# Program order for the casts and subtractions of left forms, with six buffers for forms and four for raw weights

## Chip, core and metric

The kernel runs on one core of one Trainium2 chip. The metric is the device time of one execution in microseconds, given as the median over runs; before the change it is 2421.71 us (three runs, 2420.68 to 2421.89).

## What is computed

One layer of a decoder trunk: three token mixers in parallel, a cross-attention, a gated feed-forward part and a last RMSNorm, on 1024 tokens of width 1024, in float32. The change touches only the first half of the feed-forward part:

```python
def conv_gated_ffn(h, w_up, conv_w, conv_b, w_down):
    u, v = jnp.split(h @ w_up, 2, axis=-1)          # 1024 x 1024 by 1024 x 5632
    u = causal_depthwise_conv(u, conv_w, width=3) + conv_b
    return (jax.nn.silu(u) * v) @ w_down
```

## The kernel before

Every float32 product is made of three products of rounded parts: an operand is split into a high part (`fp32r`, a cast on ScalarE) and a low part (operand minus high part, a subtraction), and high x high, high x low and low x high are summed in PSUM.

The up-projection is `ffn_up`. It treats `h @ w_up` as a two by two block product and uses a seven-product scheme: the seven right-hand forms `X` (B11, B21, T1, T2, T3, T4, B22, each as high and low part) are made from the normalised activations at the end of `trunk` and stay in SBUF. The left-hand forms come from the weights. For every block `f` of 128 columns (22 of them, D_FF/128) two raw tiles are loaded, `r1` from the u half and `r2` from the v half, 512 KB each; their halves are A11, A12, A21, A22, and GpSimd makes the sums S1, S2, S3, S4 out of them (line 1308, four per block). `left` yields one form after the other: it casts the block or sum on ScalarE (line 1315), and VectorE or GpSimd in turn subtracts (line 1316). `prod` runs the twelve matmuls of one product (line 1323).

`pair(f)` makes the products of block f and what follows them: T2 with S2 into bank `b`, T3 with S3 into half `c` of a two-bank tile `cd`, T1 with S1 into half `d`, T4 with A22 into `c` again, B22 with S4 into `d` again. VectorE reads these out between (lines 1384, 1386, 1388, 1393, 1395), then come the convolution (1397 to 1399), SiLU (1400), the gate (1401), and the left operands for the down-projection (1404, 1411 to 1413). For blocks 0 to 5 the two remaining products, A11 with B11 and A12 with B21, are made earlier by `ahead(f)`, while the end of the trunk still runs, and their results lie in DRAM (`part`); so those pairs have five products, the pairs 6 to 21 seven. After `ffn_up` comes `ffn_down`.

Buffers: the forms lie in four buffers, two of tag `whi` and two of `wlo`, taken in turn. Raw weights use two buffers of tag `raw` and, of the eight tiles r0 to r7 of another pool, r4 and r5 in the ahead stage, r2 to r5 in the pairs. r0 and r1 hold `y`, r6 and r7 hold `vt`. Before the up-projection r0 to r7 hold trunk tiles; r0 to r3 are reused there for the normalised rows from which the last right-hand forms, T3 and B22, are transposed.

The order of instructions on each engine is not written by hand. The framework schedules the program when it is built, by a simulated time line of its own: an instruction goes to its engine's queue when the simulation has it ready, and a buffer is handed out then too. Each engine then works through its queue in that fixed order. `issue_after(ins)` adds an edge that keeps what is issued inside it behind `ins` on the same engine.

Of the kernel before, what the change touches and what calls it, by code (L numbers as in the profile page):

```python
# [12 lines left out]
F32 = mybir.dt.float32  # L13
F32R = mybir.dt.float32r
# [3 lines left out]
ALU = mybir.AluOpType  # L18
# [3 lines left out]
P = 128  # L22
S = 1024
DM = 1024
NK = 8
OFF_HG, OFF_DA, OFF_RW, OFF_GATE, N_IN = 0, 2048, 3584, 5376, 8448
D_FF = 2816
NFF = 22
# [68 lines left out]
class K:  # L97
# [1194 lines left out]

    def left(self, r1, r2, which, sp):

        nc = self.nc
        V, A, G = nc.vector, nc.scalar, nc.gpsimd
        q = {f"A{n}{k + 1}": r[:, 4 * k:4 * k + 4, :] for n, r in ((1, r1), (2, r2)) if r is not None for k in range(2)}
        sums = {"S1": ("A21", "A22", ALU.add), "S2": ("S1", "A11", ALU.subtract), "S3": ("A11", "A21", ALU.subtract),  # L1300
                "S4": ("A12", "S2", ALU.subtract)}

        def get(n):
            if n not in q:
                a, b, op = sums[n]
                a, b = get(a), get(b)
                q[n] = sp.tile([P, 4, P], F32, tag=n, name=n, bufs=2 if n in ("S1", "S2") else 1)
                G.tensor_tensor(out=q[n], in0=a, in1=b, op=op)  # L1308
            return q[n]

        for n in which:
            x = get(n)
            self.nform = getattr(self, "nform", 0) + 1
            f = self.wp.tile([P, 2, 4, P], F32R, tag=("whi", "wlo")[self.nform % 2], name="wf")
            A.copy(out=f[:, 0], in_=x)  # L1315
            (V if self.nform % 2 else G).tensor_tensor(out=f[:, 1], in0=x, in1=f[:, 0].bitcast(F32), op=ALU.subtract)  # L1316
            yield f

    def prod(self, ps, f, x, start, stop):
        n = 0  # L1320
# [6 lines left out]
    def ffn_up(self, X, act, sums, part, spill):  # L1327


        nc, tc, I = self.nc, self.tc, self.I  # L1330
        V, A, G, T = nc.vector, nc.scalar, nc.gpsimd, nc.tensor
        with tc.tile_pool(name="up", bufs=1) as sp:
            col = lambda j, f: self.pc("ffn_conv_w", NFF * j + f) if j < 3 else self.pc("ffn_conv_b", f)
            nraw = itertools.count()
            u = sp.tile([P, S + 2], F32, name="u")
            G.memset(u[:, 0:2], 0.0)
            ne = part.shape[1]

            def load(m, bufs=6):
                n = next(nraw) % bufs  # L1340
                r = self.wp.tile([P, NK, P], F32, tag="raw", name="raw") if n < 2 else \
                    self.res.tile([P, NK, P], F32, tag=f"r{n + 6 - bufs}", name="raw")
                nc.sync.dma_start(out=r, in_=I["t_up"][m])
                return r

            def copy(nm, src):
                s1 = sp.tile([P, 512], F32, tag="s1", name=nm, bufs=3)
                A.copy(out=s1, in_=src)
                return s1

            def bank(f):
                return self.tps.tile([P, 512], F32, tag="t", name="ps_a") if f % 2 == 0 else \
                    self.dps.tile([P, 1024], F32, tag="d", name="ps_a")[:, 0:512]

            def ahead(f):
                forms, a = self.left(load(f, 4), None, ("A11", "A12"), sp), bank(f)
                self.prod(a, next(forms), X["B11"], True, True)
                nc.sync.dma_start(out=part[0, f], in_=copy("s1", a))
                yield
                self.prod(a, next(forms), X["B21"], False, True)  # L1360
                c = spill.tile([P, 512], F32, tag="acr", name="c11")
                A.copy(out=c, in_=a)
                nc.sync.dma_start(out=part[1, f], in_=c)
                yield

            def pair(f, rs):

                forms = self.left(*rs, ("S2", "S3", "S1", "A22", "S4") if f < ne else ("A11", "S2", "S3", "S1", "A12", "A22", "S4"), sp)
                if f < ne:
                    s1 = sp.tile([P, 512], F32, tag="s1", name="s1", bufs=3)  # L1370
                    nc.sync.dma_start(out=s1, in_=part[0, f])
                else:
                    a = self.tps.tile([P, 512], F32, tag="t", name="ps_a")
                    self.prod(a, next(forms), X["B11"], True, True)
                    s1 = copy("s1", a)
                if f < ne:
                    nc.sync.dma_start(out=u[:, 2:514], in_=part[1, f])
                vt = self.res.tile([P, S], F32, tag=f"r{6 + f % 2}", name="vt")
                b = self.mps.tile([P, 512], F32, tag="m", name="ps_b2")
                cd = self.dps.tile([P, 1024], F32, tag="d", name="ps_cd")  # L1380
                c, d = cd[:, 0:512], cd[:, 512:1024]
                u2, u3 = (sp.tile([P, 512], F32, tag=t, name=t) for t in ("u2", "u3"))
                self.prod(b, next(forms), X["T2"], True, True)
                V.tensor_tensor(out=u2, in0=b, in1=s1, op=ALU.add)
                self.prod(c, next(forms), X["T3"], True, True)
                V.tensor_tensor(out=u3, in0=c, in1=u2, op=ALU.add)
                self.prod(d, next(forms), X["T1"], True, True)
                V.tensor_tensor(out=vt[:, 512:1024], in0=d, in1=u3, op=ALU.add)
                if f >= ne:
                    self.prod(a, next(forms), X["B21"], False, True)  # L1390
                    A.copy(out=u[:, 2:514], in_=a)
                self.prod(c, next(forms), X["T4"], False, True)
                V.tensor_tensor(out=vt[:, 0:512], in0=c, in1=u2, op=ALU.add)
                self.prod(d, next(forms), X["B22"], False, True)
                V.tensor_tensor(out=u[:, 514:1026], in0=d, in1=u2, op=ALU.add)
                y = self.res.tile([P, S], F32, tag=f"r{f % 2}", name="y")
                A.activation(out=y, in_=u[:, 2:], func=AF.Identity, scale=col(2, f), bias=col(3, f))
                V.scalar_tensor_tensor(out=y, in0=u[:, 1:S + 1], scalar=col(1, f), in1=y, op0=ALU.mult, op1=ALU.add)
                V.scalar_tensor_tensor(out=y, in0=u[:, 0:S], scalar=col(0, f), in1=y, op0=ALU.mult, op1=ALU.add)
                A.activation(out=y, in_=y, func=AF.Silu)  # L1400
                V.tensor_tensor(out=y, in0=y, in1=vt, op=ALU.mult)
                q = nc.gpsimd if f >= NFF - 2 else nc.sync
                if f % 2 == 0:
                    V.tensor_tensor(out=y[:, 512:1024], in0=y[:, 0:512], in1=y[:, 512:1024], op=ALU.subtract)
                    even.append(y)
                q.dma_start(out=act[f], in_=y)
                if f % 2:
                    e = even.pop()
                    s2, s1, s4 = (self.res.tile([P, S], F32, tag=f"r{2 + n}", name="asum")[:, 0:512] if f == NFF - 1 else
                                  spill.tile([P, 512], F32, tag="acr", name="asum") for n in range(3))  # L1410
                    V.tensor_tensor(out=s2, in0=y[:, 512:1024], in1=e[:, 512:1024], op=ALU.subtract)
                    G.tensor_tensor(out=s4, in0=y[:, 0:512], in1=s2, op=ALU.subtract)
                    G.tensor_tensor(out=s1, in0=e[:, 0:512], in1=s2, op=ALU.add)
                    for n, x in enumerate((s2, s1, s4)):
                        q.dma_start(out=sums[n, f // 2], in_=x)

            even = []
            prev = None
            for f in range(ne):
                g = ahead(f)  # L1420
                next(g)
                if prev is not None:
                    next(prev)
                prev = g
            next(prev)
            rs = [load(0), load(NFF)]
            for f in range(NFF):
                nx = [load(f + 1), load(NFF + f + 1)] if f + 1 < NFF else None
                pair(f, rs)
                rs = nx  # L1430
# [200 lines left out]
```

## Time and profile before

| what | value |
|---|---|
| median of the runs | 2421.71 us (2420.68 to 2421.89) |
| profiled execution | 2418.76 us |
| its span, first to last instruction | 2417.0 us |
| mean granted clock of TensorE | 0.987 |
| PE busy | 2312.8 us, 96% |
| VectorE (DVE) busy | 1373.9 us, 57% |
| ScalarE (ACT) busy | 908.9 us, 38% |
| GpSimd (POOL) busy | 695.2 us, 29% |

The table is of one profiled execution. Busy matmul time is modelled, and neighbouring matmuls overlap in it, so starts of instructions say more than busy times. Times in the rows below are from the start of the span; the up-projection's products run from 1713 to 2188 us.

### The profile page before, as it was taken

The page shows a single profiled execution, that of the slowest core. Times are in us where ns is not written, and L with a number is a line of the kernel's source. Part 1 is how long each engine was busy: PE and PEld are TensorE (multiplying, and loading weights), DVE is VectorE, ACT ScalarE, POOL GpSimd, SP SyncE. Part 2 cuts the span into 40 slices and gives each one's busy share as a digit, 9 for nine tenths or more (in the row PEclk, how much of TensorE's full clock was granted, in tenths as well). Part 3 has the DMA queues.
Part 4 walks back from the last instruction along what each step waited for, and adds up shares of the span by engine and source line. Part 5 has one row for each costly group of instructions (what it writes and reads, how often), then busy time and mean ns, then how long its engine had stood idle before and what let it go on. Part 6 is the DMA issues. An engine that isn't in the chain of part 4 may idle for free. (4 is left out here: it accounts for less than half of the span.)

```text
span 2417.0 us, 34889 instructions
## 1 busy us (share of the span) xinstructions
PE 2312.8 (96%) x13988; PEld 1887.5 (78%) x13988; DVE 1373.9 (57%) x2098; ACT 908.9 (38%) x1430; POOL 695.2 (29%) x580
## 2 busy tenths in 40 slices
PE   7999999899999999999999999999898999998998
PEld 7877768686778787888878778888676888886886
DVE  6446374757424557454564464545547656667775
ACT  6542213131314435344442233443333333334443
POOL 1011001010111333333132440141456666551041
PEclk9999999999999999999999999999999999999999
DMA  8653312121222111111103662224243322238333
GB/s 302 221 176 125 92 58 97 58 92 45 76 70 81 53 53 37 35 60 54 44 27 121 215 213 96 96 88 135 106 165 135 111 94 105 105 142 306 97 96 122
DMA packets 110930, 266.14 MB, mean 110 GB/s; under 512 B 27248, under 2 KB 31984, under 8 KB 110768
## 3 DMA queue, kind: packets, MB, share of 16 engines
q1 hardware_dynamic: 108656, 258.25, 31.9%
q0 software_dynamic: 1248, 4.46, 0.5%
q8 instruction: 110, 1.80, 0.3%
q10 hardware_dynamic: 864, 1.20, 0.1%
q14 instruction: 52, 0.43, 0.1%
HBM read 194.40 MB, written 69.47 MB: 109 GB/s over the span
## 5 line engine op out<-in xcount | busy, mean ns | idle before, releaser
L155 PE MATMUL ps_d<-hThi,whi 128*128 128x512 f32 x1056 | 425.9, 404 | 2.0 <-DVE Ktt L261 1.6
L157 PE MATMUL ps_d<-hTlo,whi 128*128 128x512 f32 x1056 | 424.2, 402 | 0.0
L159 PE MATMUL ps_d<-hThi,wlo 128*128 128x512 f32 x1056 | 424.1, 402 | 0.0
L140 ACT CAST whi<-raw 128x1024 fp32r<-128x1024 f32 (+1 forms) x170 | 167.2, 989 | 331.4 <-PE ps_d L157 155.4
L143 DVE TENSOR_TENSOR wlo<-raw,whi 128x1024 fp32r<-128x1024 f32 (+1 forms) x125 | 156.9, 1262 | 138.2 <-ACT whi L140 138.2
L155 PEld LDWEIGHTS ps_d<-hThi,whi 128*128 128x128 f32 x1056 | 199.9, 189 | 44.5 <-issue 3.2
L157 PEld LDWEIGHTS ps_d<-hTlo,whi 128*128 128x128 f32 x1056 | 199.9, 189 | 42.8 <-issue 4.6
L159 PEld LDWEIGHTS ps_d<-hThi,wlo 128*128 128x128 f32 x1056 | 199.7, 189 | 42.7 <-issue 4.2
L143 POOL TENSOR_TENSOR wlo<-raw,whi 128x1024 fp32r<-128x1024 f32 (+1 forms) x45 | 96.8, 2150 | 433.1 <-ACT whi L140 388.4
L1490 PE MATMUL ps_dn<-wd,ap 128*128 128x512 f32 x924 | 213.2, 393 | 7.1 <-ACT wd L1466 6.7
L1490 PEld LDWEIGHTS ps_dn<-wd,ap 128*128 128x128 f32 x924 | 175.1, 190 | 45.2 <-ACT wd L1466 7.1
L1315 ACT CAST wf<-S 128x512 fp32r<-128x512 f32 x88 | 54.7, 622 | 165.0 <-PE ps_cd L1323 76.5
L1466 ACT CAST ap<-acr 128x512 fp32r<-128x512 f32 x77 | 47.9, 623 | 104.2 <-PE ps_dn L1490 93.2
L1467 DVE TENSOR_TENSOR ap<-acr,ap 128x512 fp32r<-128x512 f32 x77 | 61.4, 799 | 41.4 <-ACT ap L1466 40.6
L745 DVE CUSTOM_DVE_ANT_0 a_p<-ps_s,a_bias 128x512 f32<-128x512 f32 (+3 forms) x96 | 51.7, 553 | 50.3 <-PE ps_s L743 45.0
L159 PE MATMUL ps_d<-ohi,wlo 128*128 128x512 f32 x192 | 75.9, 395 | 3.3 <-DVE wlo L143 3.3
L1316 POOL TENSOR_TENSOR wf<-S,wf 128x512 fp32r<-128x512 f32 x44 | 62.0, 1409 | 56.1 <-ACT wf L1315 56.1
L755 ACT ACTIVATE a_p<-a_p,a_nm 128x128 f32<-128x128 f32 (+7 forms) x64 | 49.2, 770 | 75.2 <-POOL a_nm L751 57.8
L157 PE MATMUL ps_d<-olo,whi 128*128 128x512 f32 x192 | 75.8, 395 | 0.0
L155 PE MATMUL ps_d<-ohi,whi 128*128 128x512 f32 x192 | 75.8, 395 | 0.0
L1113 POOL TENSOR_SCALAR ms<-ms 128x1 f32<-128x1 f32 x30 | 11.1, 371 | 224.0 <-ACT xn L1112 146.1
L1308 POOL TENSOR_TENSOR S<-raw 128x512 f32<-128x512 f32 x44 | 58.9, 1341 | 35.6 <-DVE wf L1316 21.8
(436 smaller groups left out, 5386.3 us busy)
## 6 DMA issues: line engine op xcount, KB each, us to landing
raw<-t_in SPq DMA_DIRECT2D x66, 512.0 KB, 3.6
raw<-t_up SPq DMA_DIRECT2D x50, 512.0 KB, 3.5
th_dram<-th SPq DMA_DIRECT2D x24, 512.0 KB, 2.8
mth<-th_dram SPq DMA_DIRECT2D x24, 512.0 KB, 3.7
wdr<-ffn_w_down SPq DMA_DIRECT2D x44, 256.0 KB, 5.2
acr<-act_dram SPq DMA_DIRECT2D x44, 256.0 KB, 2.7
act_dram<-y SPq DMA_DIRECT2D x20, 512.0 KB, 2.6
acr<-sums_dram SPq DMA_DIRECT2D x33, 256.0 KB, 2.6
```

The source lines that it names most:

```text
L140: nc.scalar.copy(out=hi, in_=raw)
L143: eng.tensor_tensor(out=lo, in0=raw, in1=hi.bitcast(F32), op=ALU.subtract)
L155: nc.tensor.matmul(o, lhsT=hi[:, k, :], rhs=xhi(k, h), start=(k == 0), stop=False)
L157: nc.tensor.matmul(o, lhsT=hi[:, k, :], rhs=xlo(k, h), start=False, stop=False)
L159: nc.tensor.matmul(o, lhsT=lo[:, k, :], rhs=xhi(k, h), start=False, stop=(k == nk - 1))
L745: V.tensor_tensor_reduce(out=p_[:, a:b], in0=ps[:, 0:b - a], in1=bias[:, 1024 - n + a:1024 - n + b], op0=ALU.add, op1=ALU.max, scale=1.0, ...
L755: A.activation(out=pr[c][:, 0:n], in_=pr[c][:, 0:n], func=AF.Exp, bias=nm[:, c:c + 1], accum_out=Z[:, c:c + 1])
L1308: G.tensor_tensor(out=q[n], in0=a, in1=b, op=op)
L1315: A.copy(out=f[:, 0], in_=x)
L1316: (V if self.nform % 2 else G).tensor_tensor(out=f[:, 1], in0=x, in1=f[:, 0].bitcast(F32), op=ALU.subtract)
L1467: V.tensor_tensor(out=t[:, 1], in0=z, in1=t[:, 0].bitcast(F32), op=ALU.subtract)
L1490: T.matmul(ps[t], lhsT=a[:, p, P * t:P * t + P], rhs=w[:, q, :], start=(not behind and j == 0 and n == 0), stop=(j == NJ - 1 and n == 2), ...
```

## The change

Three things are changed. `left` now puts its casts on ScalarE in the order in which the program makes the forms, and likewise the subtractions, on VectorE and on GpSimd each for itself (`inorder`). In the pairs the forms use six buffers in turn, the four of before and r2 and r3. Raw weights use four buffers everywhere, two of tag `raw` and r4 and r5. The three activation sums of the last block, which were in r2, r3, r4, are put into r4, r5 and r2.

```diff
-    def left(self, r1, r2, which, sp):
+    def left(self, r1, r2, which, sp, slots=4):
...
         for n in which:
             x = get(n)
             self.nform = getattr(self, "nform", 0) + 1
-            f = self.wp.tile([P, 2, 4, P], F32R, tag=("whi", "wlo")[self.nform % 2], name="wf")
-            A.copy(out=f[:, 0], in_=x)
-            (V if self.nform % 2 else G).tensor_tensor(out=f[:, 1], in0=x, in1=f[:, 0].bitcast(F32), op=ALU.subtract)
+            n = self.nform % slots
+            f = self.wp.tile([P, 2, 4, P], F32R, tag=("whi", "wlo")[n % 2], name="wf") if n < 4 else \
+                self.res.tile([P, 2, 4, P], F32R, tag=f"r{n - 2}", name="wf")
+            e = self.nform % 2
+            self.inorder("A", lambda: A.copy(out=f[:, 0], in_=x))
+            self.inorder(e, lambda: (G, V)[e].tensor_tensor(out=f[:, 1], in0=x, in1=f[:, 0].bitcast(F32), op=ALU.subtract))
             yield f
+
+    def inorder(self, n, f):
+
+        last = self.__dict__.setdefault("kinds", {})
+        with self.tc.issue_after(last[n].ins) if n in last else ExitStack():
+            last[n] = f()
...
-            def load(m, bufs=6):
-                n = next(nraw) % bufs
+            def load(m):
+                n = next(nraw) % 4
                 r = self.wp.tile([P, NK, P], F32, tag="raw", name="raw") if n < 2 else \
-                    self.res.tile([P, NK, P], F32, tag=f"r{n + 6 - bufs}", name="raw")
+                    self.res.tile([P, NK, P], F32, tag=f"r{n + 2}", name="raw")
...
-                forms, a = self.left(load(f, 4), None, ("A11", "A12"), sp), bank(f)
+                forms, a = self.left(load(f), None, ("A11", "A12"), sp), bank(f)
...
-                forms = self.left(*rs, ("S2", "S3", "S1", "A22", "S4") if f < ne else ("A11", "S2", "S3", "S1", "A12", "A22", "S4"), sp)
+                forms = self.left(*rs, ("S2", "S3", "S1", "A22", "S4") if f < ne else ("A11", "S2", "S3", "S1", "A12", "A22", "S4"), sp, 6)
...
-                    s2, s1, s4 = (self.res.tile([P, S], F32, tag=f"r{2 + n}", name="asum")[:, 0:512] if f == NFF - 1 else
+                    s2, s1, s4 = (self.res.tile([P, S], F32, tag=f"r{(4, 5, 2)[n]}", name="asum")[:, 0:512] if f == NFF - 1 else
```

## Rows read from the trace of the kernel before

**Rows 1.** The page: busy time by engine; DMA issues (last number: us to landing)

```profile
PE 2312.8 (96%) x13988; PEld 1887.5 (78%) x13988; DVE 1373.9 (57%) x2098; ACT 908.9 (38%) x1430; POOL 695.2 (29%) x580
...
raw<-t_up SPq DMA_DIRECT2D x50, 512.0 KB, 3.5
```

**Rows 2.** Table by stretch, from the trunk's end to the down-projection

```profile
core 0: us, PE busy (x) PEld busy (x) DVE busy (x) ACT busy (x) POOL busy (x), PEclk, DMA share, GB/s
1713.41:1744.80 31.39, 22.51 (x105) 17.49 (x104) 24.50 (x26) 12.98 (x26) 24.04 (x21) 0.88 0.36 133
...
1771.80:1798.53 26.73, 21.91 (x90) 16.95 (x88) 9.45 (x11) 6.31 (x11) 19.27 (x15) 0.94 0.44 149
...
1864.24:1910.84 46.60, 45.14 (x195) 36.45 (x196) 31.67 (x34) 18.45 (x26) 27.35 (x19) 1.00 0.28 100
1910.84:2156.74 245.90, 245.90 (x1080) 201.90 (x1080) 152.91 (x161) 97.86 (x142) 151.71 (x106) 1.00 0.27 97
2156.74:2192.14 35.40, 25.13 (x109) 19.66 (x107) 24.03 (x31) 12.12 (x18) 9.34 (x8) 0.94 0.97 361
```

**Rows 3.** Chain that ended last, in order of time (start us, us, what)

```profile
1816.00 2.56 PE ps_b L1323 x10
...
1849.06 2.57 PE ps_b L1323 x10
...
1881.66 2.72 PE ps_cd L1323 x12
```

**Rows 4.** Time line of PE, pairs 2 and 3, rows with idle time

```profile
start us, us, engine line op out<-in xcount [idle before <-releaser]
1814.65 0.50 PE L1323 MATMUL ps_b<-T2hi,wf 128*128 128x512 f32 x1 [0.71 <-ACT wf L1315]
...
1816.00 0.73 PE L1323 MATMUL ps_b<-T2hi,wf 128*128 128x512 f32 x2 [0.62 <-POOL wf L1316]
...
1821.99 0.50 PE L1323 MATMUL ps_cd<-T3hi,wf 128*128 128x512 f32 x1 [0.71 <-ACT wf L1315]
```

**Rows 5.** Time line of ScalarE in the same stretch

```profile
1813.97 0.62 ACT L1315 CAST wf<-S 128x512 fp32r<-128x512 f32 x1 [2.05 <-PE ps_cd L1323]
```

**Rows 6.** Time line of GpSimd, 1852 to 1864 us: first two and last of seven

```profile
1852.42 1.29 POOL L1316 TENSOR_TENSOR wf<-S,wf 128x512 fp32r<-128x512 f32 x1 [3.42 <-ACT wf L1315]
1853.80 2.15 POOL L1308 TENSOR_TENSOR S<-raw 128x512 f32<-128x512 f32 x1
...
1861.80 1.74 POOL L1316 TENSOR_TENSOR wf<-S,wf 128x512 fp32r<-128x512 f32 x1
```

**Rows 7.** Time line of VectorE in the same stretch

```profile
1856.41 1.77 DVE L1316 TENSOR_TENSOR wf<-S,wf 128x512 fp32r<-128x512 f32 x1
```

**Rows 8.** Single lines of VectorE: shortest, median and longest of one, in ns

```profile
L1401 DVE TENSOR_TENSOR y<-y,vt x22: 1212/1222/2364, 1805.2 to 2191.6; 128x1024 f32<-128x1024 f32 x22
...
L1316 DVE TENSOR_TENSOR wf<-raw,wf x33: 676/693/1746, 1704.3 to 2170.3; 128x512 fp32r<-128x512 f32 x33
...
L1398 DVE SCALAR_TENSOR_TENSOR y<-u,par,y x22: 1274/1284/1972, 1800.5 to 2187.9; 128x1024 f32<-128x1024 f32 x22
```

**Rows 9.** Time lines of ScalarE and PE at the end of the trunk

```profile
1726.74 1.14 ACT L1315 CAST wf<-raw 128x512 fp32r<-128x512 f32 x2 [2.95 <-DMA raw<-t_up]
...
1733.01 1.09 PE L1254 MATMUL ps_T<-ident,t 128*128 128x128 f32 x4 [4.87 <-DVE t L1280]
...
1737.86 1.04 PE L1254 MATMUL ps_T<-ident,xk 128*128 128x128 f32 x8
```

**Rows 10.** Time lines of SP's queue, GpSimd and PE, pairs 0 and 1

```profile
1772.63 1.28 SPq L1343 DMA_DIRECT2D raw<-t_up  x3
...
1779.31 3.78 POOL L1308 TENSOR_TENSOR S<-raw 128x512 f32<-128x512 f32 x3 [4.56 <-DMA raw<-t_up]
...
1780.07 0.47 PE L1323 MATMUL ps_cd<-T1hi,wf 128*128 128x512 f32 x1 [2.17 <-DVE u L1386]
...
1785.01 0.58 PE L1323 MATMUL ps_b<-T2hi,wf 128*128 128x512 f32 x1 [1.94 <-ACT wf L1315]
```

**Rows 11.** Time line of PE in the last pair, rows with idle time

```profile
2178.59 0.47 PE L1323 MATMUL ps_cd<-T4hi,wf 128*128 128x512 f32 x1 [2.69 <-DVE vt L1388]
...
2182.45 0.47 PE L1323 MATMUL ps_cd<-B22hi,wf 128*128 128x512 f32 x1 [0.87 <-DVE vt L1393]
```

## The prediction

> **What bounds the kernel now.** I read the page first: the matmul engine (PE) is busy for 96% of the span, no other computing engine for more than 57% [rows 1]. So only stretches in which PE stands still can give time back. The chain that ended last then shows what the up-projection costs where nothing waits: a product of 12 matmuls takes 2.72 us [rows 3], so a pair of five products can take 13.60 us and one of seven 19.04 us. Against this stand the starts of successive pairs in the same view: from 1816.00 to 1849.06 two pairs of five took 33.06, 16.53 each, 2.9 us too long.
>
> The table by stretch puts the whole stage in order [rows 2]. 1713.41 to 1744.80 is the end of the trunk with the first `ahead` products; PE's instructions there are 59 matmuls, 13.4 us at 2.72 per 12, and 44 transposes, 5.7 at eight in 1.04 [rows 9]; 12.3 us are lost. 1771.80 to 1798.53 holds pairs 0 and 1: 85 matmuls, 19.3 us, four transposes, 0.5, and 6.9 lost, at a granted clock of 0.94. Pairs 2 to 5 follow until 1864.24: 65.71 us for 54.4 of work (1798.53 to 1864.24, the ends of the stretches before and behind in [rows 2]), 11.3 lost. 1864.24 to 1910.84 loses 2.4, 1910.84 to 2156.74, 1079 matmuls of 0.227, only 1.4 in 245.90: the pairs of seven run at PE's own speed, and 2156.74 to 2192.14, the last pair and the way into the down-projection, 11.2.
>
> The waits in pairs 2 to 5 have one pattern. PE's own rows [rows 4]: the T2 product of the next pair stops for 0.71 us until its cast is there, and after two matmuls 0.62 us more until its subtraction is; one product later T3 stops for 0.71. ScalarE's rows [rows 5] say why the cast was late: it had itself been idle for 2.05 us until the B22 product ended, and the one for T3 likewise until T1 ended. A cast that waits for a product waits for the buffer which that product reads. With four buffers and the forms cast out of program order, the form wanted next is cast last. That is the stall which the change goes for.
>
> **The other engines' limit.** VectorE and GpSimd do not run free of each other. A GpSimd instruction takes 1.29 us alone and up to 2.15 when VectorE is at work [rows 6]; VectorE's subtraction takes 0.68 alone [rows 8] and 1.77 in the midst of GpSimd's [rows 7]. Count the cluster from 1852.42 to 1863.54: seven GpSimd instructions of 1.29 and, of VectorE's, one L1401 (1.22 alone), one of 512 elements (0.68) and two subtractions (0.68), together 12.3 us undisturbed in 11.12. So the two work nearly one after the other, and 1 us of the union does 1.11 us of work.
>
> A pair of five needs on GpSimd four sums, 2.5 subtractions and one activation sum, 7.5 x 1.29 = 9.7; on VectorE 2.5 x 0.68 of subtractions, 2 x 1.28 of the convolution, 1.22 of the gate, 0.68 of a half-width operation = 6.2 [rows 8]. That is 15.9, and at 11.12/12.30 it takes 14.3 us. PE's floor of 13.6 can't be reached there for long; 14.3 can. A pair of seven needs 2 x 0.5 x (1.29 + 0.68) = 2.0 more, 17.9 or 16.2 us, under 19.04: no limit there.
>
> The Trainium skill ("SBUF — State Buffer", Who interferes with whom) states it harder: a VectorE instruction with two SBUF inputs and a GpSimd one that reads SBUF exclude each other for the whole instruction. By that rule the pair would need the full 15.9 us and not 14.3, and it speaks against the change: more form buffers do not make this work shorter. The cluster's 12.3 us in 11.12 side with the smaller figure.
>
> **The change part by part.**
> *Number of operations.* None is added: the same casts, subtractions, sums and loads, on the same engines (odd forms to VectorE, even to GpSimd). What moves is order and buffers.
>
> *The ahead stage, 1713 to 1772.* Still four form buffers and four of raw weights; only the order is new. Today PE stands still for 4.87 us until 1733.01, where a transpose waits for VectorE, and then runs at half clock: ten matmuls between the transposes of 1733.01 and those of 1737.86 take 4.1 us where 2.3 would do. ScalarE's casts at 1726.74 waited 2.95 for a load [rows 9]. In program order A11, A11, A12 and later A11, A12 are cast before the form whose raw tile comes late, which makes first and second products alike ready where only B11 products ran until 1737. Between nothing lost less and all of the stall with its half-clock rest (4.87 + 1.8 = 6.7) I take 3.0. The other bound is a loss: the cast queue stops at the late raw tile. Everything behind it waits as well; with five products (13.6 us) ready before it, 0 to 3 us.
>
> *Pairs 0 and 1, 1772 to 1798.* Two raw tiles of pair 1 were loaded only at 1772.63, since their buffers (r2, r3) still held trunk tiles; GpSimd waited 4.56 us for them at 1779.31 and PE 1.94 at 1785.01, with the slow clock after it [rows 10]. Now the raw tiles use only `raw` and r4, r5, which the ahead forms free earlier; r2 and r3 become the fifth and sixth form buffer and are first wanted by the fourth product. 6.9 is lost there now; the 2.17 that T1 waited for VectorE's L1386 at 1780.07 may remain. I take 5.0, with 0 and 6.9 as ends.
>
> *Pairs 2 to 5.* From 16.43 each to the floor of the two shared engines, 14.3: 4 x 2.1 = 8.4. Ends: PE's floor, 4 x 2.83 = 11.3, if a stock of six forms carries the four pairs through; and 15.9 each, 2.1, if nothing overlaps.
>
> *Later pairs.* 1.5 of the 2.4 lost to 1910.84, 0.5 of the 1.4 after; bounds 0 and 3.8 together. Four raw buffers instead of six delay loads by a pair: the tiles of pair f+2 can be fetched only when all forms of pair f are made. Those are made up to six products ahead, so before the second product of pair f; from there the load (3.5 to landing [rows 1]), two sums, cast and subtraction take 3.5 + 2.6 + 0.6 + 1.3 = 8.0 us, with a whole pair's products as cover, 13.6 to 19.0 us. On SP's queue a load that waits also holds the part and activation transfers behind it; the same cover hides that. I cost it at nothing; without the cover it would be 8.0 a pair.
>
> *The end.* The waits at 2178.59 and 2182.45 [rows 11] hang on `vt` evacuations, and the one behind the last product on that pair's post-processing, which the change doesn't touch. 0, between a gain and a loss of 3.6 (2.69 + 0.87). The moved activation sums change only names of buffers.
>
> The sum: 3.0 + 5.0 + 8.4 + 1.5 + 0.5 = 18.4 us. The profiled execution took 2418.76 (span 2417.00 and 1.76 around it), 2.95 under the median of the runs, so 2400.4 against it, and 2421.71 - 18.4 = 2403.3 against the median.
>
> **Rivals.**
> *All stalls go.* The six buffers and the early start give enough stock that PE's floor holds: 6.7 + 6.9 + 11.3 + 3.8 + 3.6 = 32.3 at most, 2389 to 2398. For it: GpSimd waits for loads before pairs 0 and 1 [rows 10] and could make their forms early. Against: the 14.3. Chance 0.15.
>
> *The shared work does not overlap at all.* Then pairs 2 to 5 give 2.1 and not 8.4: 2409.6. Against it: [rows 6, 7]. Chance 0.15, with 2407 to 2416. The rule of the Trainium skill named above would have it so.
>
> *The wait only changes its name.* S2, the first form of a pair, needs two GpSimd sums. In program order every cast stands behind it; if GpSimd's queue brings it late, pairs 2 to 5 stay at 16.4, the ahead stage at what it is, and only some 3 us of pair 1 come back: 2418.7. For it: the casts of S forms already wait for GpSimd at places. Chance 0.13.
>
> *Slower: evacuations take the stall's place.* T1 is followed by L1388, T4 by L1393, and T4 and B22 start only behind these ([rows 11]: 2.69 and 0.87; L1386 at 1780.07, 2.17, [rows 10]). Today a product of the next pair stands between. If order in the forms makes an order in the products, every pair pays twice 0.87: 22 x 1.74 = 38.3, less 18.4, is 2441.6. It decides from (18.4 + 4.8)/22 = 1.05 us a pair. Against it: with six forms, four of the next pair can lie ready while A22 and S4 wait. Chance 0.10.
>
> **How the numbers follow.** Forecast 2398 to 2407: 0.47; the rivals as said. 0.2% is 4.8 us, about what a measurement of this kernel can tell from no change: faster is under 2416.9. Faster 0.47 + 0.15 + 0.15 = 0.77, same 0.13, slower 0.10. The range 2391 to 2419 leaves out the lowest part of the first rival, the upper half of the third and the fourth.
>
> **What would show it.** Right: in pairs 2 to 5 starts of successive T2 products some 14.3 apart (16.5 now), no cast waiting for a product with PE idle behind it, GpSimd without the 4.56 wait for a load, and GpSimd and VectorE together at work nearly all of that time. Wrong: PE gaps released by VectorE's L1386, L1388 or L1393 in every pair; GpSimd waiting for raw loads in later pairs; or the idle time before 1745 grown instead of shrunk.

## The result, and the profile after it

The changed kernel takes 2444.97 us (2439.55 to 2446.55) where the kernel before took 2421.19 us in the same rounds: a ratio of 1.0093, with an interval of 1.0078 to 1.0107. The forecast was 2403.3, some 18 us faster than before; it came out about 23 us slower than before.

The profiled execution of the changed kernel took 2446.55 us, its span 2444.3, 27.3 more than before. That is 3.5 more than the medians differ (23.8), since this execution is the slowest of the four; the shares below add up to the profiled difference. On the page PE has the same 13988 matmuls, and no other engine has become full (compare [rows 1]):

```profile
PE 2322.2 (95%) x13988; PEld 1886.1 (77%) x13988; DVE 1396.7 (57%) x2098; ACT 899.8 (37%) x1430; POOL 716.3 (29%) x580
```

To see where the 27.3 us arise I cut the up-projection by pairs. A pair ends 0.227 us, one matmul, after the start of its last B22 matmul. The table by stretch of the changed kernel, cut there (first B11 matmul to the end of pair 0; pairs 1 to 5; 6 to 20; 21; behind each engine's busy time the number of its instructions):

```profile
1716.56:1796.56 80.00, 69.77 (x321) 55.24 (x319) 40.65 (x48) 31.76 (x59) 49.62 (x41) 0.94 0.47 161
1796.56:1886.38 89.82, 77.21 (x315) 58.88 (x315) 59.54 (x59) 28.15 (x39) 53.27 (x36) 0.98 0.37 119
1886.38:2198.15 311.77, 296.83 (x1261) 236.05 (x1260) 203.01 (x187) 106.56 (x164) 198.35 (x125) 0.99 0.28 98
2198.15:2213.98 15.83, 11.27 (x47) 8.21 (x45) 14.77 (x21) 5.58 (x8) 1.91 (x2) 1.00 1.05 407
```

The same cuts in the kernel before:

```profile
1713.41:1797.66 84.25, 71.26 (x321) 56.76 (x319) 42.16 (x48) 31.72 (x59) 49.66 (x41) 0.92 0.48 165
1797.66:1884.23 86.57, 77.63 (x326) 59.79 (x326) 57.61 (x60) 29.78 (x39) 54.99 (x37) 1.00 0.36 125
1884.23:2167.84 283.61, 282.68 (x1240) 231.73 (x1239) 177.17 (x185) 112.74 (x163) 176.10 (x123) 1.00 0.29 105
2167.84:2185.28 17.44, 13.87 (x59) 10.47 (x57) 13.55 (x18) 5.67 (x8) 1.91 (x2) 1.00 1.04 396
```

The first stretch gains 4.3 us, pairs 1 to 5 lose 3.3, the last pair gains 1.6, and pairs 6 to 20 lose 28.2: 283.61 before, 311.77 now. Fifteen pairs of seven products have a floor of 15 x 19.04 = 285.6, up to the products that cross a cut; before, PE was at it, now it loses some 26. (Some 5 of the 28.2 are 21 matmuls that the kernel before had made ahead of the cut, x1240 against x1261.) The granted clock there is 0.99, so the loss is standing still. The first B11 product starts 3.1 us later, which I did not follow up (in the kernels below it starts between 1708 and 1716), and the rest after the last pair is 1.4 us shorter: -4.3 + 3.3 + 28.2 - 1.6 + 3.1 - 1.4 = 27.3.

**In the pairs of five** an old wait has gone and a new one has come. PE's time line of the changed kernel, pairs 1 and 2, rows with idle time:

```profile
1808.12 0.68 PE L1332 MATMUL ps_cd<-T4hi,wf 128*128 128x512 f32 x1 [2.10 <-DVE vt L1397]
1813.52 0.50 PE L1332 MATMUL ps_cd<-B22hi,wf 128*128 128x512 f32 x1 [0.78 <-DVE vt L1402]
1817.24 0.50 PE L1332 MATMUL ps_b<-T2hi,wf 128*128 128x512 f32 x1 [0.71 <-ACT wf L1318]
```

L1397 and L1402 are the read-outs that were L1388 and L1393 before; T4 goes into the same two-bank tile from which L1397 still has to read T1. VectorE's rows show why it was late:

```profile
1804.56 1.23 DVE L1410 TENSOR_TENSOR y<-y,vt 128x1024 f32<-128x1024 f32 x1 [1.13 <-ACT y L1409]
1805.82 1.64 DVE L1413 TENSOR_TENSOR y<-y 128x512 f32<-128x512 f32 x1
1807.38 0.68 DVE L1397 TENSOR_TENSOR vt<-ps_cd,u 128x512 f32<-128x512 f32 x1
```

The read-out stands in the queue behind the gate (L1410) and the subtraction (L1413) of the pair before.

**In the pairs of seven** the matmul rows name waits of 14.7 us only, but a matmul's weights are loaded before it, and the load is what stops. The waits of PEld, pairs 6 to 20 (engine, tile and line, releaser: us in all, times, longest):

```profile
PEld ps_a L1332 <- ACT wf L1318: 12.3, 8, 2.2
PEld ps_cd L1332 <- ACT wf L1318: 6.0, 6, 1.2
PEld ps_cd L1332 <- POOL wf L1319: 3.1, 3, 1.1
PEld ps_cd L1332 <- DVE u L1395: 2.8, 5, 0.6
PEld ps_a L1332 <- DVE wf L1319: 1.6, 4, 0.4
PEld ps_b L1332 <- ACT wf L1318: 1.4, 6, 0.2
PEld ps_cd L1332 <- DVE vt L1397: 0.5, 2, 0.3
```

Together 27.7 us, about the 26 lost. Most of it is on casts, and most of that in front of B11 products (`ps_a`). One such place, ScalarE first:

```profile
2044.27 0.62 ACT L1318 CAST wf<-raw 128x512 fp32r<-128x512 f32 x1
2055.19 0.62 ACT L1318 CAST wf<-raw 128x512 fp32r<-128x512 f32 x1 [10.30 <-issue]
2055.72 0.61 ACT L1318 CAST wf<-S 128x512 fp32r<-128x512 f32 x1
2056.24 0.61 ACT L1318 CAST wf<-raw 128x512 fp32r<-128x512 f32 x1
2056.76 0.62 ACT L1318 CAST wf<-S 128x512 fp32r<-128x512 f32 x1
```

Then VectorE and PE:

```profile
2055.15 0.69 DVE L1404 TENSOR_TENSOR u<-ps_cd,u 128x512 f32<-128x512 f32 x1 [7.01 <-PE ps_cd L1332]
2055.88 0.69 DVE L1393 TENSOR_TENSOR u<-ps_b,s 128x512 f32<-128x512 f32 x1
2056.49 1.22 DVE L1319 TENSOR_TENSOR wf<-S,wf 128x512 fp32r<-128x512 f32 x1
2057.63 0.68 DVE L1395 TENSOR_TENSOR u<-ps_cd,u 128x512 f32<-128x512 f32 x1
```

```profile
2052.23 0.39 PE L1332 MATMUL ps_cd<-B22hi,wf 128*128 128x512 f32 x1
...
2056.90 0.50 PE L1332 MATMUL ps_a<-B11hi,wf 128*128 128x512 f32 x1 [1.79 <-ACT wf L1318]
...
2058.45 0.71 PE L1332 MATMUL ps_cd<-T1hi,wf 128*128 128x512 f32 x1
```

Call the pair whose B22 starts at 2052.23 f. When it ends, at 2054.95, VectorE goes through a chain: L1404 reads the temporary `u2` of f for the last time; `u2` has one buffer, so only then can L1393 write that of f+1; then, behind a subtraction that stands between in VectorE's queue, L1395 reads T3 of f+1 out of its bank, and T1 of f+1 starts at 2058.45, 3.5 us after the end of B22. (T1 goes into the other half of the two-bank tile that L1395 reads; two tiles of one bank each, which might cut the chain as well, were not tried.) T3 and B21 of f+1 are made by then, so in that time PE can only make products of f+2, and their forms are missing: the four casts from 2055.19 are A22 and S4 of f+1 and A11 and S2 of f+2, in program order. The trace names no releaser for the first of them (`issue`); what it waited for is worked out from the buffers. A pair has seven forms; the sixth form before A22 of f+1 is S4 of f, that of the very B22. So with six buffers in turn the cast of A22 waits for this B22 to end, and A11 and S2, whose own buffers are long free, wait behind it.

In the kernel before the hole is there too, and filled. PE at such a place:

```profile
2031.08 0.39 PE L1323 MATMUL ps_cd<-B22hi,wf 128*128 128x512 f32 x1
...
2033.80 0.61 PE L1323 MATMUL ps_cd<-T3hi,wf 128*128 128x512 f32 x2
...
2036.06 0.39 PE L1323 MATMUL ps_a<-B21hi,wf 128*128 128x512 f32 x1
...
2038.78 0.39 PE L1323 MATMUL ps_cd<-T1hi,wf 128*128 128x512 f32 x1
```

From the end of B22, 2033.80, to T1 it is 5.0 us, with the rest of T3 and B21 of the next pair in them. These could be kept for it, because T2 and B11 of that same next pair had filled the holes between T1, T4 and B22, their forms being cast out of turn. With the casts in order T3 and B21 are used up there (T3 from 2047.24 and B21 at 2049.51 in the changed kernel, before its B22), and nothing is left for the hole behind B22. This reading has two parts, the chain through `u2` and the form buffers; the experiments take them one by one.

### The profile page after: what moved, and what is told of

The parts are those of the page before. It is cut to its first block, busy times and chain, and to the rows that moved or that the text cites. A ratio compares the mean times of both kernels' runs of the same rounds, so it can differ in the third digit from the quotient of the medians.

```text
span 2444.3 us, 34813 instructions
## 1 busy us (share of the span) xinstructions
PE 2322.2 (95%) x13988; PEld 1886.1 (77%) x13988; DVE 1396.7 (57%) x2098; ACT 899.8 (37%) x1430; POOL 716.3 (29%) x580
## 5 line engine op out<-in xcount | busy, mean ns | idle before, releaser
L1318 ACT CAST wf<-raw 128x512 fp32r<-128x512 f32 x66 | 40.1, 619 | 160.7 <-PE ps_cd L1332 110.0
L1319 POOL TENSOR_TENSOR wf<-S,wf 128x512 fp32r<-128x512 f32 x44 | 67.8, 1547 | 59.3 <-ACT wf L1318 59.3
L1308 POOL TENSOR_TENSOR S<-raw 128x512 f32<-128x512 f32 x44 | 73.6, 1675 | 21.1 <-DMA raw<-t_up 19.6
```

The lines of the kernel that those rows point to most:

```text
L1318: self.inorder("A", lambda: A.copy(out=f[:, 0], in_=x))
L1319: self.inorder(e, lambda: (G, V)[e].tensor_tensor(out=f[:, 1], in0=x, in1=f[:, 0].bitcast(F32), op=ALU.subtract))
```

## The experiments

Each pair of medians is from one chip and one set of rounds, so kernels of different sets (after; e1 to e4; e5 to e8; e9 to e12) are compared by their ratios to before. Stage times of all profiled executions, in us, cut as above:

| kernel | to the end of pair 0 | pairs 1–5 | pairs 6–20 | pair 21 | median | ratio to before |
|---|---|---|---|---|---|---|
| before | 84.2 | 86.6 | 283.6 | 17.4 | | |
| after | 80.0 | 89.8 | 311.8 | 15.8 | 2444.97 | 1.0093 |
| e1 order alone | 79.4 | 92.9 | 304.0 | 20.7 | 2444.78 | 1.0107 |
| e2 buffers alone | 80.5 | 91.9 | 308.4 | 14.2 | 2441.38 | 1.0095 |
| e3 only casts in order | 80.3 | 89.5 | 309.3 | 18.8 | 2443.06 | 1.0102 |
| e4 after, two `u2` | 80.7 | 78.1 | 292.8 | 12.2 | 2409.84 | 0.9962 |
| e5 before, two `u2` | 86.3 | 76.4 | 285.5 | 20.0 | 2410.16 | 0.9958 |
| e6 order alone, two `u2` | 81.4 | 79.7 | 299.6 | 21.7 | 2428.60 | 1.0043 |
| e7 buffers alone, two `u2` | 80.7 | 79.6 | 287.8 | 14.2 | 2409.26 | 0.9957 |
| e8 before, four raw | 79.5 | 91.4 | 296.9 | 19.9 | 2429.92 | 1.0043 |
| e9 four raw, two `u2` | 79.3 | 78.7 | 297.5 | 19.9 | 2420.12 | 1.0010 |
| e10 order, five and five, two `u2` | 93.0 | 79.0 | 288.0 | 14.1 | 2422.37 | 1.0018 |
| e11 after, two `u2`, two `u3` | 88.3 | 69.6 | 298.9 | 11.6 | 2415.23 | 0.9986 |
| e12 before, two `u2`, two `u3` | 83.3 | 76.4 | 285.6 | 20.6 | 2411.27 | 0.9974 |

Products can cross a cut, so neighbouring columns are to be read together where one rises and the next falls.

**e1: the order alone.** The kernel before with `inorder` around casts and subtractions, and its own four form and six raw buffers.

```diff
-            A.copy(out=f[:, 0], in_=x)
-            (V if self.nform % 2 else G).tensor_tensor(out=f[:, 1], in0=x, in1=f[:, 0].bitcast(F32), op=ALU.subtract)
+            self.inorder("A", lambda: A.copy(out=f[:, 0], in_=x))
+            self.inorder(e, lambda: (G, V)[e].tensor_tensor(out=f[:, 1], in0=x, in1=f[:, 0].bitcast(F32), op=ALU.subtract))
```

> The kernel before with program order for casts and subtractions, and its own buffers (four for forms, six for raw weights). Theory A (order): forms that are cast in order but used late hold the buffers, so the products that should fill PE while VectorE reads out the two-bank tile are not ready; then this alone is at least 20 us slower than before, near or above 2441. Theory B (raw weights): four raw buffers make GpSimd wait for loads; then this stays within 8 us of before, 2413 to 2429.

2444.78 against 2418.9 us, 1.0107 [1.0091, 1.0122]: the order alone costs 26 us, as theory A had it. PEld's waits in pairs 6 to 20:

```profile
PEld ps_a L1330 <- ACT wf L1316: 16.8, 14, 1.7
```

One wait of 1.2 us in nearly every pair, for the cast in front of B11 (here L1316).

**e2: the buffers alone.** The changed kernel with no order.

```diff
-        with self.tc.issue_after(last[n].ins) if n in last else ExitStack():
+        with ExitStack():
```

> The changed kernel without the order: six buffers for forms, four for raw weights, casts and subtractions as the scheduler puts them. Theory A: at or below before, 2400 to 2424, since free order finds filling products and six buffers hold them. Theory B: as slow as the changed kernel, 2438 to 2450, with GpSimd waiting for raw loads in the pairs of seven.

2441.38 against 2418.9, 1.0095 [1.0069, 1.0120]: 22 us, in the range of theory B and not of A, and yet the whole is hardly worse than either part. PE's and GpSimd's waits, 1800 to 2190:

```profile
POOL S L1308 <- DMA raw<-t_up: 42.3, 13, 6.1
...
PE ps_cd L1332 <- DVE vt L1397: 13.6, 6, 3.1
```

PE waits here for the read-out before T4, and GpSimd for raw weights, as theory B said; whether that second wait costs anything is for e7 to tell. Two parts that cost 26 and 22 us alone and 24 together do not add; it looks like one slack, which each of them uses up.

**e3: only the casts in order.**

```diff
-        with self.tc.issue_after(last[n].ins) if n in last else ExitStack():
+        with self.tc.issue_after(last[n].ins) if n in last and n == "A" else ExitStack():
```

> The changed kernel with the order kept for the casts on ScalarE alone, subtractions free. Theory A: the casts hand out the order of the buffers' use, so it is as slow as the changed kernel within 6 us, 2439 to 2451. If the subtractions on GpSimd behind late sums were the cause, it comes back to before, 2415 to 2427. Theory B: as slow as the changed kernel as well.

2443.06 against 2418.9, 1.0102 [1.0082, 1.0123]. The time tells little, since with these buffers no order at all (e2) is as slow. The lengths of single pairs tell more: pairs 6 to 9 take 23.1, 21.2, 19.4 and 19.4 us here, 23.0, 21.2, 21.0 and 19.3 in the changed kernel, and 18.6, 21.8, 17.6 and 20.2 in e2. So the order of the casts sets how the pairs run; the subtractions follow them.

**e4: the changed kernel with a second buffer for `u2`.** This goes at the chain and leaves every part of the change in place.

```diff
-                u2, u3 = (sp.tile([P, 512], F32, tag=t, name=t) for t in ("u2", "u3"))
+                u2, u3 = (sp.tile([P, 512], F32, tag=t, name=t, bufs=n) for t, n in (("u2", 2), ("u3", 1)))
```

> The changed kernel with two buffers for u2 instead of one. In the trace of the changed kernel T1 of a pair waits for u3, u3 for u2 and u2 (one buffer) for the read-out behind B22 of the pair before. Theory A in the form that this chain of read-outs is what PE now waits for: 8 to 25 us faster than the changed kernel, 2420 to 2437. If the chain is only late because of raw loads (theory B) or forms: no change, 2441 to 2449.

2409.84 against 2418.9, 0.9962 [0.9949, 0.9975]. A second buffer of 256 KB turns 23 us slower into 9 us faster, more than the 8 to 25 us that theory A gave it. Pairs 1 to 5 and 6 to 20:

```profile
1791.64:1869.72 78.08, 72.84 (x304) 58.53 (x303) 60.45 (x58) 28.07 (x39) 55.75 (x35) 0.96 0.40 132
1869.72:2162.53 292.81, 288.38 (x1261) 235.78 (x1260) 217.43 (x188) 105.30 (x163) 209.82 (x124) 1.00 0.30 105
```

and VectorE at a place like that above:

```profile
2041.22 0.68 DVE L1393 TENSOR_TENSOR u<-ps_b,s 128x512 f32<-128x512 f32 x1
...
2043.02 0.67 DVE L1395 TENSOR_TENSOR u<-ps_cd,u 128x512 f32<-128x512 f32 x1
2046.25 0.69 DVE L1404 TENSOR_TENSOR u<-ps_cd,u 128x512 f32<-128x512 f32 x1 [2.55 <-PE ps_cd L1332]
```

L1393 and L1395 of the next pair now run 5 and 3 us ahead of L1404, and T1 follows B22 directly (2046.05, B22's product ending at the same time). PE needs no product of pair f+2 there, and the wait that bore the cast's name is gone though the casts keep their order.

**e5: the kernel before with the same second buffer.** Only the `u2` line.

> The kernel before with two buffers for u2, nothing else. Theory C (one buffer for u2 ties each pair's T1 to the read-out behind B22 of the pair before, and PE needs ready products of the pair after next to fill that time; before has them, the changed kernel does not): pairs 6 to 20 are at PE's own speed already, so a gain only in pairs 1 to 5, 2405 to 2420. Theory D (order and buffers cost by themselves, u2 is a gain of its own of some 35 us): 2380 to 2395.

2410.16 against 2419.09, 0.9958 [0.9942, 0.9974]. The old kernel gains 9 us from it, all in pairs 1 to 5 (86.6 to 76.4), which were those that the change was after. Its pairs of seven were at their floor and stay there (285.5), as theory C said; the 35 us of theory D are not there.

**e6 and e7: order alone and buffers alone, each with two `u2`.** The edits of e1 and e2 with the `u2` line.

> Program order alone with the buffers of before (four, six), and two buffers for u2. Theory C: the 26 us which order alone cost come back, 2400 to 2422. If the casts in order cost because four buffers are too few for them, whatever u2 does: 2430 to 2445, PE still waiting for casts before B11.

> Six form buffers and four raw ones without the order, and two buffers for u2. Theory C: the 22 us of the buffers alone come back, 2400 to 2422, and PE no longer waits for VectorE before T4. Theory B (four raw buffers make GpSimd wait for loads): 2428 to 2442, with GpSimd's 42 us of waits for raw loads left.

Order with four form buffers: 2428.6 against 2419.09, 1.0043 [1.0029, 1.0058]; buffers without order: 2409.26, 0.9957 [0.9942, 0.9972]. The second is as theory C said. The first lies between its two ranges: `u2` takes some 15 us off e1, and the rest stays. Against e5 the order costs 18 us with four form buffers; with six it costs nothing (e4's ratio 0.9962 against e7's 0.9957). PEld's waits in pairs 6 to 20 of e6:

```profile
PEld ps_a L1330 <- ACT wf L1316: 17.1, 15, 1.2
```

The same wait as in e1, untouched by `u2`: with four buffers in turn a cast waits for the product of the fourth form before it. e7 shows the other side, GpSimd from 1800 to 2170:

```profile
POOL S L1308 <- DMA raw<-t_up: 53.5, 18, 5.8
```

GpSimd waits 53.5 us for raw weights, more than in e2, and PE loses almost nothing by it (pairs 6 to 20: 287.8).

**e8 and e9: only four raw buffers, with one and two `u2`.**

```diff
-                n = next(nraw) % bufs
+                n = next(nraw) % 4
...
-                    self.res.tile([P, NK, P], F32, tag=f"r{n + 6 - bufs}", name="raw")
+                    self.res.tile([P, NK, P], F32, tag=f"r{n + 2}", name="raw")
```

> The kernel before with four raw buffers instead of six, form buffers and order as before. Theory B: four raw buffers are what six form buffers cost, 2434 to 2448. Theory C, in which raw tiles are early enough: within 8 us of before, 2411 to 2427.

> The kernel before with four raw buffers and two for u2. Theory C: four raw buffers make GpSimd wait for loads some 40 us in all but that is hidden once u2 has two buffers, so the 11 us of four raw buffers come back and it is at 2405 to 2415, as the kernel before with two u2 (2410). Theory B (the wait for loads costs by itself): 2418 to 2428.

e8: 2429.92 against 2419.09, 1.0043 [1.0028, 1.0058]. e9: 2420.12 against 2420.12, 1.0010 [0.9997, 1.0024]. Four raw buffers cost 11 us in the old kernel and, against e5, 10 by the medians or 13 by the ratios with two `u2`: here `u2` is not the cause. e8 lies above theory C's range and below B's; in e9 C missed and B has it. e9's pairs 6 to 20 take 297.5 where e5's take 285.5. PE's and GpSimd's waits in e8, 1800 to 2170:

```profile
POOL S L1308 <- DMA raw<-t_up: 42.6, 18, 3.8
...
PE ps_b L1323 <- POOL wf L1316: 6.6, 7, 1.7
```

Raw weights come late, the sum S2 and its subtraction with them, and PE's largest wait is in front of T2. With six form buffers (e7) nothing is lost; that the forms are then ready far enough ahead to take the delay is the likely reason, not one that a run shows by itself. In the changed kernel GpSimd waits only 9.5 us for raw weights between 1800 and 2190.

**e10: five form and five raw buffers, order, two `u2`.** The split between the two.

```diff
-            def load(m):
-                n = next(nraw) % 4
+            def load(m, bufs=5):
+                n = next(nraw) % bufs
...
-                    self.res.tile([P, NK, P], F32, tag=f"r{n + 2}", name="raw")
+                    self.res.tile([P, NK, P], F32, tag=f"r{n + 6 - bufs}", name="raw")
...
-... "A12", "A22", "S4"), sp, 6)
+... "A12", "A22", "S4"), sp, 5)
```

> Program order, five form buffers, five for raw weights, two for u2. With four form buffers this was 2428.6, with six (and four raw) 2409.8. Theory of slots (in order, four forms that wait for their turn fill the buffers): between them or at the lower, 2405 to 2422. If it was the raw buffers or something else in the six that helped: 2425 to 2432.

2422.37 against 2420.12, 1.0018 [1.0007, 1.0028]. At the upper end of the range that the theory of slots gave. Pairs 6 to 20 take 288.0, no more than with six (e4, 292.8); the loss is ahead, 93.0 us to the end of pair 0 where e4 takes 80.7. SP's queue, GpSimd and PE there:

```profile
1773.65 0.33 SPq L1352 DMA_DIRECT2D raw<-t_up  x1
...
1777.83 3.70 POOL L1308 TENSOR_TENSOR S<-raw 128x512 f32<-128x512 f32 x3 [15.37 <-DMA raw<-t_up]
...
1783.45 0.80 PE L1332 MATMUL ps_b<-T2hi,wf 128*128 128x512 f32 x1 [9.84 <-ACT wf L1318]
```

A raw tile for pair 0 is loaded only at 1773.65. The fifth raw buffer is r3, which is still a tile of the trunk; that this is why the load is late is read from the code and was not tried.

**e11 and e12: a second buffer for `u3` too**, in e4 and in e5 (with `s1` in two buffers instead of three, for room).

```diff
-                u2, u3 = (sp.tile([P, 512], F32, tag=t, name=t) for t in ("u2", "u3"))
+                u2, u3 = (sp.tile([P, 512], F32, tag=t, name=t, bufs=2) for t in ("u2", "u3"))
```

> The changed kernel with two buffers each for u2 and u3 (and two instead of three for s1). If u3's one buffer ties the pairs as u2's did: 3 to 12 us below the changed kernel with two u2 (2409.8), 2398 to 2407. If the tie was u2's alone: 2406 to 2414.

> The kernel before with two buffers each for u2 and u3 (two for s1). Tie through u3 too: 2398 to 2407. Through u2 alone: 2406 to 2414, as with two u2 (2410).

2415.23 against 2420.12, 0.9986 [0.9975, 0.9998], and 2411.27, 0.9974 [0.9964, 0.9984]: no better than with `u2` alone, and e11 some 6 us worse by the ratios, which is not explained. Two things changed at once, and a gain from `u3` could hide a loss from `s1`; but in e12 each of the pairs 1 to 20 takes what it takes in e5 within 0.05 us, so in the old kernel neither matters there. What the chain needed was `u2`.

Six form buffers beside six raw ones were not tried, so what six form buffers do by themselves is not shown.

## Why the prediction was wrong

*Later pairs.* This is the step that failed. It read 245.90 us without idle time as "run at PE's own speed" and so as a stage in which nothing could be lost but the cover of a load. But PE ran through because T3 and B21 of the next pair stood in the hole between B22 and T1, and they were left for it because casts went out of turn. The change takes away what filled the hole, and the profile of before showed no wait there because it was filled. In place of 2.0 us of gain pairs 6 to 20 lost 28.2. e4 shows that the hole is the one chain through `u2`: with it open, 19.0 of the 28.2 come back with no other edit (311.8 to 292.8; some 5 of the rest are the matmuls that crossed the cut before), and in all some 32 us (ratio 1.0093 to 0.9962).

*Four raw buffers at nothing.* The cover that the step named, a pair's products, exists only while the forms are made a pair ahead. With four form buffers the price is 11 us (e8), with six and two `u2` nothing that can be measured (e7 against e5). What share they have in the 23 us of the changed kernel, which has one `u2`, no run parts.

*Pairs 2 to 5, 8.4 us.* Cut behind B22 they took 70.5 us before and 70.0 after. The stretch that the step read, 1798.53 to 1864.24, is by that cut pairs 1 to 4, and these went from 65.7 to 74.1: nothing of the 8.4 came. The cause that the step named, four buffers with casts out of order, was the releaser in the rows, and removing it only brought the read-outs forward: in pairs 1 to 5 of the changed kernel PE waits 7.3 us for L1397 and L1402 and 3.7 for casts. The aim of 14.3 us a pair was near in size: in e5 pairs 1 to 4 take 15.41, 13.60, 16.19 and 13.60, 14.7 on average, with the old order and the old form buffers. So 6.9 of the 8.4 us were to be had, by another edit. That 14.7 is no proof of the limit, though: in this stretch GpSimd has 27 instructions and not the 30 of four pairs, and by the undisturbed durations of the prediction they and VectorE's instructions without a PSUM input come to 59.5 us; the two engines were at work on them for 54.8 of the 58.8 us. The Trainium skill ("SBUF — State Buffer", Who interferes with whom), by whose rule the prediction's sum is not to be shortened, is on the high side here as well, 59.5 us against 54.8.

*The ahead stage and pairs 0 and 1, 3.0 + 5.0.* From the first B11 product to the end of pair 0 4.3 us came back, as forecast in kind, but that product started 3.1 us later; pair 1 gave 3.7 back to the read-outs (16.12 to 19.82).

*The rival on the other side* had the right sign, and 2441.6 is near the 2444.97, but for half the reason, so that the nearness is luck in part. Read-outs did take the stall's place in pairs 1 to 5, 7.3 us in five pairs, 1.5 each where 1.74 was said. In pairs 6 to 20, where most was lost, PE's weight loads wait 19.7 us of 27.7 for casts and 3.3 for VectorE's read-outs. And most of the 18.4 us of gain that it counted against the cost was not there. The argument against it, that four forms of the next pair can lie ready, failed on the turn of the buffers: forms that lie ready in program order are of no use when the one that would fill the hole stands behind one that waits.

*Rivals that fell.* That all stalls go, that the shared work is the limit, and that the wait only changes its name all left the later pairs alone or counted a gain there, and all missed.

Open: why buffers alone (e2) make PE wait for L1397 rather than for casts, and why the first product starts 3.1 us later. The order in the queues comes from the framework's own time line, and no run here takes that apart.

## What to carry to other kernels

A stretch in which the bounding engine never waits is not free of limits: look for the single-buffered temporary that ties one iteration to the next, work out how long that tie is, and name the work that covers it before changing the order or buffers that supply this work. The releaser that a wait names is only the last link; giving the temporary two buffers brought here, with one line, half of what reordering the casts was meant to bring (9 of 18.4 us). The Trainium skill ("Perfetto Trace Analysis", Optimization Strategy) says that a gap that repeats on the engine that should be full can mean that there isn't room for the next tile; the runs agree (some 32 us for a second `u2`), with the addition that the buffer that was short was not that of the tile waited for.

## What the runs showed of the hardware

PE's standing still shows fully only in its weight loads: in pairs 6 to 20 of the changed kernel the waits of PEld add to 27.7 us and those of the matmuls to 14.7, while some 26 us were lost against the floor. And an engine's waits by themselves say nothing of their price: GpSimd waited 42.6 us for raw weights in e8, a kernel that is 11 us slower than before, and 53.5 in e7, which is no slower than e5.
